# Hybrid decoder layer on one core: first loads on two queues, table load ahead, decay differences on ScalarE

## The chip, the cores and the metric

The kernel runs on one core of one Trainium2 chip. The metric is the time of one execution on the device, in microseconds (us). The engines are named as in the profile: PE (TensorE matmuls), PEld (its weight loads), DVE (VectorE), ACT (ScalarE), POOL (GpSimd) and SP (SyncE, which issues transfers).

## The reference

One decoder layer over 512 tokens of width 1024, in float32:

```python
h = x
h = h + 0.5 * swiglu(rmsnorm(h, g1), w_gate_up, w_down)          # first feed-forward, 2816 wide
proj = rmsnorm(h, g) @ w_in                                      # mixers
y_a = short_conv_branch(b, c, v); y_b = mamba2_branch(z, xbc, dt)
h = h + (sigmoid(g_a) * y_a + sigmoid(g_b) * y_b) @ w_mix_out
h = h + memory_cross_attention(rmsnorm(h, gx), rmsnorm(mem, gm))
h = h + 0.5 * swiglu(rmsnorm(h, g2), ...)                        # second feed-forward
out = rmsnorm(h, gf)
```

The part of the mamba2 branch that the change touches, per head and per chunk of 128 tokens, with `acs` the running sum of `dt * a` (never rising, since a is negative):

```python
seg = acs[..., :, None] - acs[..., None, :]
decay = exp(where(causal, seg, -inf))
y_diag = einsum('bcgls,bcgkls,bcsgkp->bclgkp', C_B, decay, x)    # C_B: C times B, per group
```

## The kernel before, in words

Activations lie with channels on the 128 partitions and the 512 tokens along the row. Every float32 product is made of three matmuls of rounded parts: each operand is split into `hi` and `lo` (`split`, L102: ACT copies to `hi`, DVE subtracts to get `lo`), and a product is hi·hi + hi·lo + lo·hi (L130 to L132 in `job`, L212 to L215 in `mm3`). Weights come from HBM in pieces of 128x1024 through `load_w` (L109): the transfer to tile `wr` is issued by SP, then ACT and DVE split it to `wh` and `wl`. Each of the three tags has three buffers. The order of the instructions on each engine is set when the kernel is built, by a scheduler; on the chip each engine goes through its own list in order.

**Start.** SP issues, in this order: `prm` (all small parameters, L85), the input tile `h0` (L173), the first weight piece in two halves of 128x512 (L115), `h1`, `h2` (L176), the second weight piece (L115), `h3` to `h7` (L179) and the constants `con` (L180). `gained` (L134) multiplies each `h[k]` by its gain and splits it: ACT makes `uh` (L139), DVE `ul` (L140). The first matmuls (L212) need `uh0` and the first half of `wh`. The norm itself (`rms`, L143) is applied behind the matmuls.

**Mixers.** For each of 4 groups of 8 heads, `ssd_out` (L513) goes through 4 pairs of heads (i = 0 to 3). For each head of a pair a transfer by SP spreads the 512 values of `acs` over all partitions into a tile `m` (L520, from the scratch tensor `acd`; four buffers, so the heads of pairs 2 and 3 reuse those of pairs 0 and 1). POOL subtracts `acs` by partition (L522), ACT takes Relu of the negated difference (L525) and then Exp of its negative (L526), DVE multiplies by the masked C·B tile `cb` (L527), and eight small matmuls of 64x128 a pair use it (L539). Three more matmuls (L544) make the part that comes from earlier chunks, scaled by `ea`, which ACT makes with Exp (L533). DVE joins the parts in `yg` (L548, L550), multiplies by the gate (L556), and after four pairs `rms` sums the squares (L150 on ACT, L154 on DVE) and PE adds them over partitions (L158). Matmuls of the next projections (called projection matmuls here, output `pj`) stand between these small ones on PE. The pairs 2 and 3 of a group, with its norm, are called its late half.

Of the kernel before, what the change touches and what calls it, by code (L numbers as in the profile page):

```python
# [62 lines left out]
def layer(ctx: ExitStack, tc: tile.TileContext, a, out):  # L63
# [18 lines left out]
        return psp.tile([P, T], F32, tag=tag, name=nm(tag), bufs=PJ if tag == "pj" else 8 - PJ)  # L82

    prm = cst.tile([P, NCOL], F32, tag="prm", name="prm")
    nc.sync.dma_start(out=prm, in_=a["prm"])  # L85
    h = [hp.tile([P, T], F32, tag=f"h{k}", name=f"h{k}") for k in range(KD)]
    xv = a["xT"].rearrange("(k p) t -> k p t", p=P)
    con = cst.tile([P, 3, P], F32, tag="con", name="con")
    ident, ones, triu = con[:, 0, :], con[:, 1, :], con[:, 2, :]
    eps = cst.tile([P, 1], F32, tag="eps", name="eps")  # L90
    V.memset(eps, EPS)


    cst.tile([P, 8], F32, tag="fill", name="fill")
    small = lambda tag, n, bufs: cst.tile([P, n], F32, tag=tag, name=nm(tag), bufs=bufs)

    ahead = []
# [11 lines left out]
    def load_w(src, n, parts=1):  # L109
        if ahead:  # L110
            return ahead.pop(0)
        raw, hi, lo = ring("wr", F32), ring("wh"), ring("wl")
        for i in range(parts):
            c = slice(i * n // parts, (i + 1) * n // parts)
            nc.sync.dma_start(out=raw[:, c], in_=src[:, c])  # L115
            split(raw[:, c], hi[:, c], lo[:, c])
        return hi, lo
# [16 lines left out]
    def gained(src, gname, k, pool, tag="u", bufs=8, n=T):  # L134

        hi = pool.tile([P, n], F32R, tag=tag + "h", name=nm("uh"), bufs=bufs)
        lo = pool.tile([P, n], F32R, tag=tag + "l", name=nm("ul"), bufs=bufs)
        g = pc(gname, k)
        S.activation(out=hi, in_=src, func=AF.Copy, scale=g)  # L139
        V.scalar_tensor_tensor(out=lo, in0=src, scalar=g, in1=hi, op0=ALU.mult, op1=ALU.subtract)  # L140
        return hi, lo
# [28 lines left out]
        S.copy(out=r, in_=p2[:, :n_tok])  # L170
        return r

    nc.sync.dma_start(out=h[0], in_=xv[0])  # L173
    first = [load_w(a["w_gu1"][0][:, :8 * P], 8 * P, 2)]
    for k in range(1, 3):
        nc.sync.dma_start(out=h[k], in_=xv[k])  # L176
    first.append(load_w(a["w_gu1"][0][:, 8 * P:], 8 * P))
    for k in range(3, KD):
        nc.sync.dma_start(out=h[k], in_=xv[k])  # L179
    nc.sync.dma_start(out=con, in_=a["con"].rearrange("p (a b) -> p a b", a=3))  # L180
    ahead.extend(first)

    up = ctx.enter_context(tc.tile_pool(name="up", bufs=1))
# [4 lines left out]
    def ffn(gname, wgu, wd, fin=None):  # L188
# [2 lines left out]
        ts = ExitStack()  # L191
        tp = ts.enter_context(tc.tile_pool(name=nm("tp"), bufs=1, reuse_waits="tile"))
        tp.tile([P, 48], F32, tag="lag", name=nm("lag"))
        u = [gained(h[k], gname, k, up) for k in range(KD)]
        tq = []
        s = {}

# [186 lines left out]
    with tc.tile_pool(name="mx", bufs=1, reuse_waits="tile") as mx:  # L384
# [128 lines left out]
        def ssd_out(g, ct, xs, cb, xdt, prev):  # L513
            yg = []
            for i in range(4):
                h0 = 8 * g + 2 * i
                ms = []
                for hh in range(2):
                    m = mt("m", MB)
                    DQ.dma_start(out=m, in_=acd_h[h0 + hh].partition_broadcast(P))  # L520
                    m4 = m.rearrange("p (c l) -> p c l", c=NC)
                    G.tensor_tensor(out=m4, in0=m4,  # L522
                                    in1=acs[:, (h0 + hh) * NC:(h0 + hh + 1) * NC].unsqueeze(2)
                                    .to_broadcast([P, NC, P]), op=ALU.subtract)
                    S.activation(out=m, in_=m, func=AF.Relu, scale=-1.0)  # L525
                    S.activation(out=m, in_=m, func=AF.Exp, scale=-1.0)  # L526
                    V.tensor_tensor(out=m, in0=m, in1=cb, op=ALU.mult)  # L527
                    ms.append(m)
                ea = mt("ea", 2)
                for hh in range(2):  # L530
                    DQ.dma_start(out=ea[64 * hh:64 * hh + 64, :],
                                 in_=acd_h[h0 + hh].partition_broadcast(64))
                S.activation(out=ea, in_=ea, func=AF.Exp)  # L533
                yd = ps("ss")
                for c in range(NC):
                    cs = slice(c * P, (c + 1) * P)
                    for hh in range(2):
                        q0 = (2 * i + hh) * 64
                        TE.matmul(yd[64 * hh:64 * hh + 64, cs], xdt[c][:, q0:q0 + 64], ms[hh][:, cs],  # L539
                                  start=True, stop=True)  # L540
                yo = ps("ss")
                for c in range(1, NC):
                    cs = slice(c * P, (c + 1) * P)
                    TE.matmul(yo[:, cs], prev[c - 1][:, i * P:(i + 1) * P], ct[:, cs],  # L544
                              start=True, stop=True)
                V.tensor_tensor(out=ea[:, P:], in0=yo[:, P:], in1=ea[:, P:], op=ALU.mult)
                y = mt("yg", 4)
                V.scalar_tensor_tensor(out=y, in0=xs[i], scalar=pc("ssm_d", 4 * g + i), in1=yd,  # L548
                                       op0=ALU.mult, op1=ALU.add)
                V.tensor_tensor(out=y[:, P:], in0=y[:, P:], in1=ea[:, P:], op=ALU.add)  # L550
                yg.append(y)
            return yg
# [365 lines left out]
```

## Time and profile before

| what | value |
|---|---|
| time, median of 3 runs | 1591.48 us (1591.46 to 1591.81) |
| time of the profiled execution | 1592.54 us |
| its span, first to last instruction | 1590.8 us |
| PE busy | 1557.4 us (98%) |
| DVE, ACT, POOL busy | 1056.0, 733.7, 52.7 us |
| granted clock of TensorE, mean | 0.995 |

The busy time of an engine is what its instructions cover; waits, branches and the issuing of transfers are not counted. A share of the whole span hides what single stretches do, so the stretches where PE stands still are read one by one.

### The profile page before, as it was taken

What the parts mean: (1) busy time and instruction counts of PE and PEld (TensorE: products, weight loads), DVE (VectorE), ACT (ScalarE), POOL (GpSimd) and SP (SyncE); (2) the same over time, 40 slices, a digit from 0 to 9 for tenths busy, and PEclk for the clock granted to TensorE, in tenths of its full rate; (3) what the DMA queues carried; (4) which work ended last, traced back from release to release, by engine and by line L of the source; (5) the groups of instructions that cost most, each with busy time, mean ns of one, the idle gap of its engine ahead of it and who ended that gap; (6) DMA issues with size and microseconds to landing.
All of it is one profiled execution on the core that took longest, in us unless ns stands there. A gap on an engine that the chain in (4) does not pass through costs nothing.

```text
span 1590.8 us, 20744 instructions
## 1 busy us (share of the span) xinstructions
PE 1557.4 (98%) x8253; PEld 1318.0 (83%) x8253; DVE 1056.0 (66%) x1502; ACT 733.7 (46%) x1008; POOL 52.7 (3%) x54
## 2 busy tenths in 40 slices
PE   7999999999989999899999999999999999999997
PEld 6888988987778777787888888888888898998986
DVE  6856856777684877958565544565556876666765
ACT  7432433445768593765332233344344642342343
POOL 0000000002020200201000000000000000000000
PEclk9999999999999999999999999999999999999999
DMA  5432333245242423323242322235204233233221
GB/s 196 133 93 93 98 112 100 66 132 188 93 133 80 138 75 117 122 93 108 78 146 93 105 94 93 95 105 185 93 27 130 83 120 107 93 95 111 86 62 71
DMA packets 53920, 168.70 MB, mean 106 GB/s; under 512 B 6320, under 2 KB 6832, under 8 KB 53824
## 3 DMA queue, kind: packets, MB, share of 16 engines
q1 hardware_dynamic: 51952, 161.03, 31.8%
q0 software_dynamic: 1584, 5.31, 0.9%
q8 instruction: 64, 1.05, 0.3%
q10 hardware_dynamic: 288, 1.05, 0.2%
q14 instruction: 32, 0.26, 0.1%
HBM read 163.10 MB, written 4.26 MB: 105 GB/s over the span
## 4 chain that ended last, share of the span: by engine, by line
PE 55%; DVE 2%; issue 1%; ACT 1%; DMA 0%; DVEq 0%; ACTq 0%
PE pj L132 12%; PE pj L131 12%; PE pj L130 12%; PE pj L212 5%; PE pj L214 5%; PE pj L215 5%; DMA ea<-acd 0%; PE pj L676 0%; PE pj L678 0%; PE pj L677 0%; PE ss L539 0%; DVE wl L104 0%; PE ss L758 0%; ACT wh L103 0%; PE ss L721 0%
## 5 line engine op out<-in xcount | busy, mean ns | idle before, releaser
L103 ACT CAST wh<-wr 128x1024 fp32r<-128x1024 f32 (+2 forms) x250 | 243.6, 975 | 479.9 <-PE pj L131 332.2
L104 DVE TENSOR_TENSOR wl<-wr,wh 128x1024 fp32r<-128x1024 f32 (+2 forms) x250 | 282.0, 1129 | 112.6 <-ACT wh L103 111.0
L130 PE MATMUL pj<-uh,wh 128*128 128x512 f32 (+1 forms) x712 | 281.2, 395 | 0.0
L132 PE MATMUL pj<-uh,wl 128*128 128x512 f32 (+1 forms) x712 | 280.4, 394 | 0.0
L131 PE MATMUL pj<-ul,wh 128*128 128x512 f32 (+1 forms) x712 | 279.5, 393 | 0.0
L212 PE MATMUL pj<-uh,wh 128*128 128x512 f32 (+1 forms) x416 | 153.3, 369 | 8.3 <-ACT wh L103 7.1
L132 PEld LDWEIGHTS pj<-uh,wl 128*128 128x128 f32 (+1 forms) x712 | 133.9, 188 | 29.0 <-issue 0.7
L130 PEld LDWEIGHTS pj<-uh,wh 128*128 128x128 f32 (+1 forms) x712 | 133.8, 188 | 28.6 <-issue 0.9
L131 PEld LDWEIGHTS pj<-ul,wh 128*128 128x128 f32 (+1 forms) x712 | 134.0, 188 | 27.8
L214 PE MATMUL pj<-ul,wh 128*128 128x512 f32 (+1 forms) x416 | 152.4, 367 | 0.0
L215 PE MATMUL pj<-uh,wl 128*128 128x512 f32 (+1 forms) x416 | 151.9, 366 | 0.0
L130 PE MATMUL pj<-sh,wh 128*128 128x512 f32 x346 | 135.3, 391 | 0.1
L131 PE MATMUL pj<-sl,wh 128*128 128x512 f32 x346 | 135.1, 390 | 0.2
L132 PE MATMUL pj<-sh,wl 128*128 128x512 f32 x346 | 134.8, 390 | 0.0
L212 PEld LDWEIGHTS pj<-uh,wh 128*128 128x128 f32 x416 | 78.6, 189 | 22.6 <-ACT wh L103 7.1
L214 PEld LDWEIGHTS pj<-ul,wh 128*128 128x128 f32 x416 | 79.0, 190 | 13.1 <-DVE ul L140 0.5
L215 PEld LDWEIGHTS pj<-uh,wl 128*128 128x128 f32 x416 | 78.5, 189 | 12.8 <-DVE wl L104 0.2
L131 PEld LDWEIGHTS pj<-sl,wh 128*128 128x128 f32 x346 | 65.0, 188 | 14.5 <-DVE sl L104 1.5
L130 PEld LDWEIGHTS pj<-sh,wh 128*128 128x128 f32 x346 | 65.0, 188 | 14.0 <-ACT sh L103 0.9
L132 PEld LDWEIGHTS pj<-sh,wl 128*128 128x128 f32 x346 | 65.0, 188 | 13.4
L352 DVE SCALAR_TENSOR_TENSOR dn<-pj,r 128x512 f32<-128x512 f32 x47 | 32.4, 690 | 57.2 <-PE pj L132 56.9
L381 DVE SCALAR_TENSOR_TENSOR cv<-cx,prm,cv 128x511 f32<-128x511 f32 (+2 forms) x72 | 62.1, 866 | 3.4 <-ACT cv L378 3.1
(278 smaller groups left out, 3088.6 us busy)
## 6 DMA issues: line engine op xcount, KB each, us to landing
wr<-in_w_in SPq DMA_DIRECT2D x80, 512.0 KB, 3.2
wr<-in_w_gu SPq DMA_DIRECT2D x63, 512.0 KB, 3.8
wr<-in_w_d SPq DMA_DIRECT2D x32, 512.0 KB, 3.5
db<-in_w_gu SPq DMA_DIRECT2D x24, 512.0 KB, 3.8
m<-acd SPq DMA_DIRECT2D x32, 256.0 KB, 3.9
wr<-in_w_os SPq DMA_DIRECT2D x32, 256.0 KB, 3.1
wr<-in_w_d SPq DMA_DIRECT2D x16, 384.0 KB, 3.2
ea<-acd SPq DMA_DIRECT2D x32, 128.0 KB, 4.4
```

Source lines behind the costliest of these rows:

```text
L103: S.copy(out=hi, in_=src)
L104: V.tensor_tensor(out=lo, in0=src, in1=hi, op=ALU.subtract)
L130: TE.matmul(pt, hi[:, s_], xh, start=(k == 0), stop=False)
L131: TE.matmul(pt, hi[:, s_], xl, start=False, stop=False)
L132: TE.matmul(pt, lo[:, s_], xh, start=False, stop=(k == nk - 1))
L212: TE.matmul(pt, hi[:, c], xh, start=start and k == 0, stop=False, skip_group_check=True)
L214: TE.matmul(pt, hi[:, c], xl, start=False, stop=False, skip_group_check=True)
L215: TE.matmul(pt, lo[:, c], xh, start=False, stop=stop and k == 3, skip_group_check=True)
L352: V.scalar_tensor_tensor(out=dn, in0=pd, scalar=0.5, in1=r, op0=ALU.mult, op1=ALU.mult)
L381: V.scalar_tensor_tensor(out=acc[:, d:], in0=x[:, :T - d], scalar=pc(wname, j0 + j), in1=acc[:, d:], op0=ALU.mult, op1=ALU.add)
```

## The change

The start: SP issues `prm`, then the first quarter of the first 128x2048 of weights, `h1`, the second quarter, `h4`, the third and fourth quarters, `h5` to `h7` and `con`. ACT issues `h0`, then loads its function table for a copy of one value per partition into a spare tile, then issues `h2` and `h3`. The quarters are split between the `gained` steps (after k = 0, 2, 3 and 5). The mixers: POOL's subtraction is gone; ACT makes Relu(acs - m) in four pieces of 128x128 per head, each with its own column of `acs` as the bias by partition.

```diff
-    nc.sync.dma_start(out=prm, in_=a["prm"])
     xv = a["xT"].rearrange("(k p) t -> k p t", p=P)
+    S.dma_start(out=h[0], in_=xv[0])
+    nc.sync.dma_start(out=prm, in_=a["prm"])
...
-    cst.tile([P, 8], F32, tag="fill", name="fill")
+    warm = cst.tile([P, 8], F32, tag="fill", name="fill")[:, 0:1]
+    S.activation(out=warm, in_=eps, func=AF.Copy, scale=eps)
...
-    nc.sync.dma_start(out=h[0], in_=xv[0])
-    first = [load_w(a["w_gu1"][0][:, :8 * P], 8 * P, 2)]
-    for k in range(1, 3):
-        nc.sync.dma_start(out=h[k], in_=xv[k])
-    first.append(load_w(a["w_gu1"][0][:, 8 * P:], 8 * P))
-    for k in range(3, KD):
+    def load_first(src):
+        return ring("wr", F32), ring("wh"), ring("wl"), src
+    def piece(t, i, eng):
+        raw, hi, lo, src = t
+        c = slice(i * 512, (i + 1) * 512)
+        eng.dma_start(out=raw[:, c], in_=src[:, c])
+        return lambda: split(raw[:, c], hi[:, c], lo[:, c])
+    f0, f1 = load_first(a["w_gu1"][0][:, :1024]), load_first(a["w_gu1"][0][:, 1024:])
+    jobs = [piece(f0, 0, nc.sync)]
+    nc.sync.dma_start(out=h[1], in_=xv[1])
+    S.dma_start(out=h[2], in_=xv[2])
+    jobs.append(piece(f0, 1, nc.sync))
+    S.dma_start(out=h[3], in_=xv[3])
+    nc.sync.dma_start(out=h[4], in_=xv[4])
+    jobs += [piece(f1, 0, nc.sync), piece(f1, 1, nc.sync)]
+    for k in range(5, KD):
         nc.sync.dma_start(out=h[k], in_=xv[k])
     nc.sync.dma_start(out=con, in_=a["con"].rearrange("p (a b) -> p a b", a=3))
+    first = [f0[1:3], f1[1:3]]
...
-        u = [gained(h[k], gname, k, up) for k in range(KD)]
+        u = []
+        for k in range(KD):
+            u.append(gained(h[k], gname, k, up))
+            if jobs and k in (0, 2, 3, 5):
+                jobs.pop(0)()
...
-                    m4 = m.rearrange("p (c l) -> p c l", c=NC)
-                    G.tensor_tensor(out=m4, in0=m4,
-                                    in1=acs[:, (h0 + hh) * NC:(h0 + hh + 1) * NC].unsqueeze(2)
-                                    .to_broadcast([P, NC, P]), op=ALU.subtract)
-                    S.activation(out=m, in_=m, func=AF.Relu, scale=-1.0)
+                    for c in range(NC):
+                        col = (h0 + hh) * NC + c
+                        S.activation(out=m[:, c * P:(c + 1) * P], in_=m[:, c * P:(c + 1) * P],
+                                     func=AF.Relu, scale=-1.0, bias=acs[:, col:col + 1])
                     S.activation(out=m, in_=m, func=AF.Exp, scale=-1.0)
```

The scheduler orders all engines anew. ACT at the start, before (L139 is `uh`, L103 the split of weights):

```order
L139 ACT_TABLE_LOAD
L139 ACTIVATE uh_120<-h_71,prm 128x512
L103 CAST wh_85<-wr_84 128x512 x2
L139 ACTIVATE uh_124<-h_72,prm 128x512
L139 ACTIVATE uh_128<-h_73,prm 128x512
L150 ACTIVATE sq_202<-h_71 128x512
```

and after (L87, L188 and L190 are the transfers, L142 is `uh`, L106 the split):

```order
L87 DMA h_70<-in_xT 128x512
L97 ACT_TABLE_LOAD
L97 ACTIVATE fill<-eps 128x1
L188 DMA h_72<-in_xT 128x512
L190 DMA h_73<-in_xT 128x512
L142 ACTIVATE uh_116<-h_70,prm 128x512
L106 CAST wh_86<-wr_85 128x512
L142 ACTIVATE uh_122<-h_71,prm 128x512
L142 ACTIVATE uh_126<-h_72,prm 128x512
L106 CAST wh_86<-wr_85 128x512
```

The table load stands ahead of everything that waits for data, and `uh` of `h1` and `h2` now stands before the second split of weights.

ACT in the late half of group 0, before (L525 Relu, L526 Exp, L533 Exp of `ea`):

```order
L525 ACTIVATE m_3926<-m_3926 128x512
L526 ACT_TABLE_LOAD
L526 ACTIVATE m_3926<-m_3926 128x512
L525 ACTIVATE m_3932<-m_3932 128x512
L525 ACTIVATE m_3959<-m_3959 128x512
L526 ACTIVATE m_3932<-m_3932 128x512
L533 ACTIVATE ea_3938<-ea_3938 128x512
L526 ACTIVATE m_3959<-m_3959 128x512
L525 ACTIVATE m_3965<-m_3965 128x512
```

and after (L543 Relu, L545 Exp, L552 Exp of `ea`):

```order
L543 ACTIVATE m_3938<-m_3938,keep 128x128 x4
L543 ACTIVATE m_3946<-m_3946,keep 128x128
L545 ACT_TABLE_LOAD
L545 ACTIVATE m_3938<-m_3938 128x512
L543 ACTIVATE m_3946<-m_3946,keep 128x128 x3
L552 ACTIVATE ea_3954<-ea_3954 128x512
L545 ACTIVATE m_3946<-m_3946 128x512
L543 ACTIVATE m_3975<-m_3975,keep 128x128 x4
L543 ACTIVATE m_3983<-m_3983,keep 128x128
L545 ACTIVATE m_3975<-m_3975 128x512
```

Five small Relu pieces stand before the first Exp, where one large Relu stood. In the whole program ACT's table loads go from 74 to 59.

PE at the first use of pair 2 in group 0, before (L539 uses `m`, L544 is the part of earlier chunks, `pj` are projection matmuls):

```order
L130 MATMUL pj_4125<-uh_3262,wh_4127 128x512
L131 MATMUL pj_4125<-ul_3263,wh_4127 128x512
L539 MATMUL ss_3942<-m_3926,xdt_3817 64x128
L544 MATMUL ss_3951<-ct_3501,prev_3823 128x128
L544 MATMUL ss_3951<-ct_3501,prev_3836 128x128
L544 MATMUL ss_3951<-ct_3501,prev_3850 128x128
L132 MATMUL pj_4125<-uh_3262,wl_4128 128x512
L539 MATMUL ss_3942<-m_3932,xdt_3817 64x128
```

and after (L558 uses `m`, L563 is the part of earlier chunks):

```order
L135 MATMUL pj_4145<-uh_3266,wl_4148 128x512
L558 MATMUL ss_3958<-m_3938,xdt_3821 64x128
L563 MATMUL ss_3967<-ct_3505,prev_3827 128x128
L563 MATMUL ss_3967<-ct_3505,prev_3840 128x128
L563 MATMUL ss_3967<-ct_3505,prev_3854 128x128
L133 MATMUL pj_4145<-uh_3270,wh_4147 128x512
L134 MATMUL pj_4145<-ul_3271,wh_4147 128x512
L135 MATMUL pj_4145<-uh_3270,wl_4148 128x512
L133 MATMUL pj_4145<-uh_3274,wh_4147 128x512
L134 MATMUL pj_4145<-ul_3275,wh_4147 128x512
L135 MATMUL pj_4145<-uh_3274,wl_4148 128x512
L133 MATMUL pj_4145<-uh_3278,wh_4147 128x512
```

Seven projection matmuls stand where one stood. Counted from PE's list, the projection matmuls before the first `m` matmul of pair 2; between it and that of the pair's second head; before pair 3; between its two heads; before the sums of squares (L158):

| group | before | after |
|---|---|---|
| 0 | 23, 1, 10, 1, 34 | 22, 7, 3, 7, 21 |
| 1 | 23, 1, 10, 1, 34 | 25, 6, 4, 6, 24 |
| 2 | 23, 1, 10, 1, 34 | 23, 4, 7, 4, 21 |
| 3 | 20, 3, 2 (with both heads), 3, 27 | 21, 4, 7, 4, 23 |

The number of matmuls is the same in both kernels. In the first feed-forward L158 comes after 61 matmuls instead of 63.

## Rows read from the trace of the kernel before

**Rows 1.** The page, busy time by engine.
```profile
PE 1557.4 (98%) x8253; PEld 1318.0 (83%) x8253; DVE 1056.0 (66%) x1502; ACT 733.7 (46%) x1008; POOL 52.7 (3%) x54
```
**Rows 2.** Waits of PE: who waited for whom, total us, times, longest.
```profile
PE ss L539 <- DVE m L527: 8.3, 4, 2.7
PE pj L212 <- ACT wh L103: 7.1, 1, 7.1
PE ss L158 <- DVE sq L154: 4.6, 3, 1.7
```
**Rows 3.** Windows: length, busy PE, PEld, DVE, ACT, POOL; clock, DMA share, GB/s.
```profile
447.50:450.91 3.41, 3.41 (x21) 2.96 (x21) 2.33 (x4) 3.38 (x6) 0.00 (x0) 0.50 0.00 0
```
**Rows 4.** Timeline of the start: start us, us, engine line op [idle before <-releaser].
```profile
1.66 0.90 SPq L115 DMA_DIRECT2D wr<-in_w_gu  x2
...
4.09 1.28 ACT L139 ACT_TABLE_LOAD   x1 [4.09 <-DMA h<-in_xT]
...
6.43 0.62 ACT L103 CAST wh<-wr 128x512 fp32r<-128x512 f32 x1 [0.33 <-DMA wr<-in_w_gu]
```
**Rows 5.** Timeline of the start, ACT and PE after the first matmuls.
```profile
8.51 0.62 ACT L103 CAST wh<-wr 128x512 fp32r<-128x512 f32 x1 [1.46 <-DMA wr<-in_w_gu]
9.17 1.39 ACT L139 ACTIVATE uh<-h,prm 128x512 fp32r<-128x512 f32 x2
...
9.94 0.79 PE L212 MATMUL pj<-uh,wh 128*128 128x512 f32 x1 [1.19 <-ACT uh L139]
...
11.75 0.63 PE L212 MATMUL pj<-uh,wh 128*128 128x512 f32 x1
```
**Rows 6.** Windows: the start, and the first feed-forward.
```profile
4.00:6.00 2.00, 0.00 (x0) 0.00 (x0) 0.00 (x0) 1.90 (x2) 0.00 (x0) 1.00 0.70 137
30.00:50.00 20.00, 20.00 (x90) 16.51 (x89) 19.03 (x31) 15.25 (x20) 0.00 (x0) 1.00 0.25 78
```
**Rows 7.** Timeline, late half of group 0: POOL, DVE, ACT and PE.
```profile
440.64 5.25 POOL L522 TENSOR_TENSOR m<-m,keep 128x512 f32<-128x512 f32 x4 [38.74 <-DMA m<-acd]
...
439.14 0.55 DVE L550 TENSOR_TENSOR yg<-yg,ea 128x384 f32<-128x384 f32 x1
...
440.68 1.41 DVE L550 TENSOR_TENSOR yg<-yg,ea 128x384 f32<-128x384 f32 x1
...
446.35 0.68 DVE L527 TENSOR_TENSOR m<-m,cb 128x512 f32<-128x512 f32 x1
...
443.66 0.63 ACT L526 ACTIVATE m<-m 128x512 f32<-128x512 f32 x1
444.20 1.13 ACT L525 ACTIVATE m<-m 128x512 f32<-128x512 f32 x2
...
447.18 0.41 PE L539 MATMUL ss<-m,xdt 128*64 128x128 f32 x2 [2.67 <-DVE m L527]
```
**Rows 8.** Groups of DVE by form (count, busy us, mean ns): taps beside POOL's work, and later.
```profile
L381 DVE SCALAR_TENSOR_TENSOR cv<-cx,prm,cv 128x510 f32<-128x510 f32 x24 | 23.8, 993 | 0.1
...
L381 DVE SCALAR_TENSOR_TENSOR c<-v,prm,c 128x510 f32<-128x510 f32 x8 | 6.0, 750 | 0.3
```
**Rows 9.** Groups of ACT by form: Silu with and without a column, Relu, Exp.
```profile
L443 ACT ACTIVATE xs<-cv,prm 128x512 f32<-128x512 f32 x16 | 11.5, 721 | 1.0 <-DVE cv L381 0.9
...
L509 ACT ACTIVATE z<-z 128x512 f32<-128x512 f32 x16 | 10.1, 632 | 0.8 <-DVE z L508 0.7
...
L525 ACT ACTIVATE m<-m 128x512 f32<-128x512 f32 x32 | 19.4, 621 | 25.6 <-POOL m L522 25.6
...
L424 ACT ACTIVATE m<-m 128x128 f32<-128x128 f32 x1 | 0.3, 310 | 0.0
```
**Rows 10.** Timeline, DVE before PE's first wait in groups 1 and 3.
```profile
544.90 1.39 DVE L527 TENSOR_TENSOR m<-m,cb 128x512 f32<-128x512 f32 x1
...
739.35 0.69 DVE L527 TENSOR_TENSOR m<-m,cb 128x512 f32<-128x512 f32 x1 [0.85 <-ACT m L526]
```
**Rows 11.** Windows: up to the norm of group 1.
```profile
548.00:566.00 18.00, 16.33 (x96) 12.91 (x96) 17.56 (x23) 15.55 (x22) 5.37 (x4) 1.00 0.44 146
```

## The prediction

> **What bounds the kernel.** I read the page first: PE is busy 1557.4 us of the span of 1590.8 [rows 1], so only some 33 us can be won without taking matmuls away. The waits of PE tell where most of them are [rows 2]: 7.1 us before the first matmul, 8.3 us in four waits (one a group) for the decay tile `m` at the start of pair 2, 4.6 us in three waits for the sum of squares at the end of groups 0 to 2. The windows show a cost beside these: three stretches in the mixers, 3.41 us each, in which the granted clock is 0.50, the lower of TensorE's two levels (1.2 of 2.4 GHz) [rows 3] (the row is the first; the others begin at 467.98 and 662.54). Two of the three follow a wait for squares, one the wait of 2.67 us. Each costs 3.41 x 0.5 = 1.7 us, together 5.1. The change works on all of these.
>
> **The start.** ACT's table load of 1.28 us stood behind the wait for `h0`, at 4.09 [rows 4]. Moving it ahead gives nothing by itself: after `uh` the engine stood still 0.33 us more until the first half of the weights had landed, at 6.4, and the split and the first matmul follow that landing. What counts is when the first quarter lands. It is issued second on SP instead of third; two issues took 0.90 us [rows 4], so it goes out 0.45 us sooner. Lower bound 0, since the same bytes (`prm`, `h0`, quarter) must arrive. Upper bound: it lands together with `h0` at 4.09; then `uh` (0.70, half of the 1.39 of two [rows 5]) goes first, the split starts at 4.79 instead of 6.43, 1.6 us sooner. I take 0.45, nearest to the row of the same transfer. ACT's own two later issues (some 0.45 us each, after the table load that may begin at once) end before 4.1, so the wait for `h0` hides them; without that cover they would cost 0.9.
>
> Next, PE stood 1.19 us before 9.94 [rows 5]: `uh` of `h1` had been queued behind the second split (8.51 to 9.13), itself late by 1.46 us. Now `h1` is issued ahead of the second quarter and its `uh` stands ahead of that split, so it can start about when that quarter landed, at 8.5 instead of 9.17: 0.66 us. The dense stream starts that much sooner, so I count 0.7 for both steps (they are one path, not two). The first matmuls go at the lower clock (one still takes 0.63 us at 11.75 [rows 5], while later 90 of them take 20.00 us, 0.22 each [rows 6]). If the clock rises sooner by the same 0.7, half of that is won again: 0.4; if sooner by a stretch as long as those of [rows 3], 1.7. **Start: 1.1 us, between 0 and 4.5** (1.6 + 1.2 + 1.7). The upper end is unlikely to last: between 30 and 50 us DVE is busy 19.03 of 20 us [rows 6], so matmuls that come sooner soon meet DVE's splits and sums.
>
> The issuing engines are one more question. Between 4 and 6 us the 16 DMA engines were busy 0.70 of the time although many transfers had been issued [rows 6]; a second queue that filled them would bring the first quarter 2.0 x 0.30 = 0.6 us sooner still, a total of 1.7 at the start. The Trainium skill, DMA: Bandwidth & Descriptors, section "Issuing engines are not separate DMA queues", says against this that transfers from several engines interleave on the same DMA engines and that only issue time is saved. By that rule the start stays at 1.1 us; no trace here shows two queues at the start.
>
> **POOL's subtraction.** What it costs is not mainly its own time. While POOL ran its four subtractions, 440.64 to 445.89, an add on DVE of 128x384 took 1.41 us; the same add before it took 0.55 [rows 7]. Over all groups the taps of 128x510 took 993 ns in the mixers and 750 ns where POOL was idle [rows 8]. So DVE reached the multiply of `m` only at 446.35, though ACT's Exp had ended at 444.29 [rows 7]: PE waited 2.1 us for DVE's backlog, not for the decay chain. Without POOL, DVE's four steps between 440.68 and 446.35 need at most 0.55 + 3 x 0.75 = 2.8 us, and DVE is free at 443.5.
>
> **ACT's pieces.** No row shows a Relu of 128x128 with a column as bias. A 128x128 activation takes 0.31 us, and a column adds 721 - 632 = 89 ns [rows 9], so 0.40 alone; one behind the other they overlap by about 0.1 (two Relus of 0.62 take 1.13 [rows 7]), so 0.3 each, 0.31 to be safe. Bounds 0.25 and 0.52 (a whole Relu, one behind the other). Per tile 4 x 0.31 = 1.24 instead of 0.52, over 32 tiles about 23 us more ACT; 15 table loads fewer at 1.28 [rows 4] give 19 back. ACT is busy 46% [rows 1], so the totals don't matter; the chain of a tile does. In group 0 the transfer had landed at 440.64. Five pieces 1.55, table 1.28, Exp 0.63: 444.1, as before (444.29). The multiply (0.68) ends at 444.8 instead of 447.03. PE comes 0.2 sooner (22 matmuls instead of 23) and waits 0.5 instead of 2.67: 2.1 us won. Group 2 is the same pattern: 2.3. In group 1 the multiply itself took 1.39 instead of 0.68 [rows 10] and PE comes two matmuls later: 1.5. In group 3 DVE waited 0.85 for ACT [rows 10], so ACT's chain sets the time and only 0.5 is won. Sum 6.4.
>
> For the later heads ACT gets slower: each tile takes 0.72 more, four tiles 2.9, less the 1.3 of POOL's first subtraction (a quarter of 5.25 [rows 7]) that came before: the fourth Exp comes 1.6 later. The new order puts seven, three and seven matmuls between the heads, where one, ten and one stood: 17 x 0.22 = 3.7 us instead of 2.6. By the same reckoning as above PE then waits about 0.2, 0.45 and 0.15 us at these three places in group 0; I take 0.6 a group, 2.5 in all. **First waits: 6.4 - 2.5 = 3.9 us**, between 0 (the pieces give back all) and 8.3.
>
> The queues: nothing on POOL is behind the subtraction that PE needs. ACT now waits itself for the transfer of `m`; behind it stand only the Exps, and ACT stood idle there for POOL before, 25.6 us in all [rows 9]. On SP the `m` transfers of the next group go behind one weight transfer; they are needed late, after the norm.
>
> **The norm's waits.** Up to L158 of group 1 DVE is busy 17.56 of 18 us with 5.37 of POOL beside it [rows 11]. At twice the length beside POOL, half of 5.37, 2.7 us, goes. But L158 also stands earlier: 38 matmuls after pair 2's first instead of 46 in group 0, 40 in group 1, 36 in group 2: 1.8, 1.3 and 2.2 us. The difference is 0.9 + 1.4 + 0.5 = **2.8 us** of the 4.6 [rows 2]; bounds -1.3 (half of the relief of 8.1 us in three groups reaches the sum, against 5.3 that L158 comes sooner) and 4.6.
>
> **The clock.** With the waits mostly under 1 us I take two of the three slow stretches away: **3.4 us**, between 0 and 5.1. Seven waits [rows 2] went with three slow stretches, so not every wait of this size brings one, and no row says what one under 1 us does; I leave one.
>
> **Sum.** 1.1 + 3.9 + 2.8 + 3.4 = 11.2 us. The profiled execution took 1592.54, so 1581.3; the median of the runs is 1.06 lower, so **1580.2 us**. About 0.2% (3.2 us) is what a measurement of this kernel can tell from no change.
>
> **Rivals.**
> *Two queues carry more.* The first quarter and `h1` land with `h0`, and the clock rises sooner: 4.5 instead of 1.1 at the start. For it: DMA engines not full [rows 6]; against: DVE right behind. 1576.8 us. Chance 0.18.
> *The wait moves.* Only half of DVE's relief reaches the sums of squares, because L158 stands earlier, and the slow stretches stay: 1.1 + 3.9 - 1.3 = 3.7 us, 1587.8; with one slow stretch more 2.0, 1589.5. For it: DVE has little free time in the late half even so [rows 11]; against: 8.1 us of relief is more than the 5.3. Chance 0.14.
> *ACT becomes the bound, slower than before.* Place: the 16 pieces of a late half, on the way to the last `m`. If a piece costs 0.52, as much as a Relu of four times its size, the 16 take 3.4 us more than at 0.31, and PE waits for each of them: 13.4 in four groups. The slow stretches then stay, so 13.4 - 11.2 + 3.4 = 5.6 us slower, 1597.1. It decides at 0.31 + (11.2 - 3.4) / 64 = 0.43 us a piece. Against: the 0.31 that a 128x128 takes even alone without a column [rows 9]. Chance 0.04.
> *The start alone doesn't move* (the quarter lands at 6.4 as before): 1581.3 us, inside the forecast.
>
> **Chances and range.** Forecast 0.64, rivals as said. The range for 8 in 10 reaches over the first rival and most of the second: 1573.5 to 1588.5. Faster by over 0.2% 0.85 (forecast and first rival, and a little of the second), within 0.2% 0.11, slower 0.04.
>
> **What would show it.** Right: first matmul near 6.6 us; PE's waits for `m` under 1 us each, their sum under 4.5; taps of 128x510 near 750 ns in the mixers too; one slow stretch or none in the mixers; PE's first matmul of pair 2 released by ACT's chain rather than by DVE's backlog. Wrong: pieces of over 0.45 us, waits at L158 over 2 us, or a clock at 0.50 in three places again.

## The result, and the profile after

| what | before | after |
|---|---|---|
| median of 5 runs | 1591.48 us (1589.77 to 1592.26) | 1583.25 us (1580.82 to 1585.28) |
| profiled execution, its span | 1592.54, 1590.8 us | 1583.25, 1581.5 us |

The ratio is 0.9948 (95% interval 0.9933 to 0.9963): 8.2 us faster by the medians, 9.3 us between the two profiled executions. I forecast 1580.2 and 11.2 us, in a range from 1573.5 to 1588.5. The sign and most of the mechanism hold. The sum does not come about term by term as I wrote it.

The page, busy time of the changed kernel, answers to [rows 1]:

```profile
PE 1556.1 (98%) x8253; PEld 1316.7 (83%) x8253; DVE 1036.4 (66%) x1503; ACT 733.2 (46%) x1091; POOL 10.4 (1%) x22
```

POOL's 42 us of subtractions are gone, DVE does the same work in 19.6 us less, and ACT's total did not move, since fewer table loads pay for the pieces. PE's waits answer to [rows 2] (total us, times, longest):

```profile
PE pj L232 <- ACT wh L106: 7.1, 1, 7.1
PE pj L135 <- DVE wl L107: 3.5, 1, 3.5
PE ss L558 <- DVE m L546: 2.7, 5, 1.5
...
PE ss L479 <- ACT ct L463: 0.9, 1, 0.9
...
PE ss L161 <- DVE sq L157: 0.4, 1, 0.4
```

The waits for `m` fell from 8.3 to 2.7 us. Those for squares at the ends of groups 0 to 2 fell from 4.6 to nothing worth a row: the 0.4 that is listed stands in the first feed-forward, at 23 us, where the kernel before has no such wait. The first wait of 7.1 is what it was. Two rows are new: 3.5 us for `wl` at 655.5, and 0.9 us at 460.9 for `ct`, which ACT makes with Silu for the next group. The windows for the clock answer to [rows 3]:

```profile
447.50:450.91 3.41, 3.41 (x27) 2.66 (x28) 2.90 (x6) 3.38 (x6) 0.00 (x0) 1.00 0.66 222
659.00:662.41 3.41, 3.41 (x8) 2.73 (x9) 3.41 (x4) 3.38 (x7) 0.00 (x0) 0.50 0.60 208
1054.95:1058.37 3.42, 3.34 (x15) 3.34 (x16) 3.42 (x10) 2.03 (x5) 0.00 (x0) 0.50 0.49 158
```

The stretch of [rows 3] is at full clock now. One stretch at 0.50 is left in the mixers, and it stands right behind the new wait for `wl`. Another has come at 1055, behind two waits of 1.26 and 0.66 us for the split of the memory (`mnh`, `mnl`, operands of the cross attention) that the kernel before has too, without a fall.

At the start I expected the first matmul near 6.6 us. The timeline of the changed kernel answers to [rows 4, 5]:

```profile
1.18 1.28 ACT L97 ACT_TABLE_LOAD   x1 [1.18 <-PEq L928]
...
4.01 0.72 ACT L142 ACTIVATE uh<-h,prm 128x512 fp32r<-128x512 f32 x1 [1.24 <-DMA h<-in_xT]
...
6.38 0.62 ACT L106 CAST wh<-wr 128x512 fp32r<-128x512 f32 x1 [1.66 <-DMA wr<-in_w_gu]
...
7.05 0.80 PE L232 MATMUL pj<-uh,wh 128*128 128x512 f32 x1 [7.05 <-ACT wh L106]
7.57 1.34 ACT L142 ACTIVATE uh<-h,prm 128x512 fp32r<-128x512 f32 x2 [0.57 <-DMA h<-in_xT]
...
8.50 0.64 PE L232 MATMUL pj<-uh,wh 128*128 128x512 f32 x1
...
10.54 0.40 PE L234 MATMUL pj<-ul,wh 128*128 128x512 f32 x1
```

The table load is out of the way and `uh` is done 1.3 us sooner, but ACT now waits 1.66 us for the first quarter instead of 0.33. The quarter went out 0.48 us sooner and its split began at 6.38 instead of 6.43. The second step worked: `uh` of `h1` comes ahead of the second split, and the matmul that stood still for 1.19 us in [rows 5] follows without a gap. The last row is the first matmul at the faster pace (0.40 us in the list, 0.23 from one start to the next, where 0.63 and 0.43 stood before it). In the kernel before, the first at that pace is the 13th, 3.6 us later:

```profile
14.18 0.40 PE L215 MATMUL pj<-uh,wl 128*128 128x512 f32 x1
```

In the late half of group 0 the chain of [rows 7] looks like this:

```profile
438.28 1.58 ACT L543 ACTIVATE m<-m,keep 128x128 f32<-128x128 f32 x5 [5.07 <-DMA m<-acd]
...
441.17 0.63 ACT L545 ACTIVATE m<-m 128x512 f32<-128x512 f32 x1
...
441.83 0.69 DVE L546 TENSOR_TENSOR m<-m,cb 128x512 f32<-128x512 f32 x1 [0.61 <-ACT m L545]
...
442.68 0.40 PE L558 MATMUL ss<-m,xdt 128*64 128x128 f32 x2 [0.33 <-DVE m L546]
```

Five pieces in a row take 1.58 us (I had 1.55). Now DVE waits 0.61 us for ACT, where PE waited for DVE's backlog before. The taps (the steps of the short convolution, L381 before, L401 now) answer to [rows 8]:

```profile
L401 DVE SCALAR_TENSOR_TENSOR cv<-cx,prm,cv 128x510 f32<-128x510 f32 x24 | 17.9, 745 | 0.1
```

That is the 750 ns that I expected, down from 993.

The new wait, on the timeline at the border from group 2 to 3:

```profile
652.57 1.06 ACT L106 CAST wh<-wr 128x1024 fp32r<-128x1024 f32 x1 [0.25 <-PE pj L134]
...
655.08 2.73 DVE L401 SCALAR_TENSOR_TENSOR cv<-cx,prm,cv 128x510 f32<-128x510 f32 x4
...
657.72 1.22 DVE L107 TENSOR_TENSOR wl<-wr,wh 128x1024 fp32r<-128x1024 f32 x1
...
658.99 0.79 PE L135 MATMUL pj<-uh,wl 128*128 128x512 f32 x1 [3.48 <-DVE wl L107]
```

`wh` was there at 653.63. DVE had other work in its list first, four taps among it, and began the subtraction for `wl` at 657.72. PE stood still from 655.51 on.

### The profile page after: what moved, and what is told of

Read it like the earlier page. It is cut to its first block, busy times and chain, and to the rows that moved or that the text cites. A ratio compares the mean times of both kernels' runs of the same rounds, so it can differ in the third digit from the quotient of the medians.

```text
span 1581.5 us, 20708 instructions
## 1 busy us (share of the span) xinstructions
PE 1556.1 (98%) x8253; PEld 1316.7 (83%) x8253; DVE 1036.4 (66%) x1503; ACT 733.2 (46%) x1091; POOL 10.4 (1%) x22
## 4 chain that ended last, share of the span: by engine, by line
PE 92%; DVE 3%; DMA 2%; ACT 2%; issue 1%; DVEq 0%; SPq 0%; ACTq 0%
PE pj L135 19%; PE pj L134 19%; PE pj L133 19%; PE pj L232 9%; PE pj L234 9%; PE pj L235 9%; DMA ea<-acd 1%; PE ss L558 1%; PE ss L509 1%; DVE wl L107 1%; ACT wh L106 1%; PE ss L563 1%; PE pj L697 0%; PE pj L696 0%; PE pj L695 0%
## 5 line engine op out<-in xcount | busy, mean ns | idle before, releaser
L106 ACT CAST wh<-wr 128x1024 fp32r<-128x1024 f32 (+2 forms) x251 | 243.8, 972 | 501.9 <-PE pj L134 357.0
L106 ACT CAST wh<-sa 128x1024 fp32r<-128x1024 f32 x24 | 25.3, 1054 | 71.1 <-PE pj L234 39.9
```

The lines of the kernel that those rows point to most:

```text
L106: S.copy(out=hi, in_=src)
```

## The experiments

**The start alone.** The kernel before with the start of the change; in the mixers POOL subtracts as before.

```diff
+    S.dma_start(out=h[0], in_=xv[0])
+    S.activation(out=warm, in_=eps, func=AF.Copy, scale=eps)
...
+    jobs += [piece(f1, 0, nc.sync), piece(f1, 1, nc.sync)]
```

> The start of the change alone (three queues' issues, table load ahead, quarters); POOL keeps its subtraction and ACT its whole Relu. The order of all instructions behind the first feed-forward's start is that of the kernel before. Theory (the start is worth what the trace of the changed kernel shows at the same matmul, 1.8 us, and the rest of the gain is the mixers'): 1.8 us faster than before, 1.2 to 2.4; first matmul at 7.1 as before, no wait before the matmul of h1's `uh`, waits for `m` 8.3 us in four and for squares 4.6 in three. Rival (the start's gain is used up by DVE's backlog in the first feed-forward): under 0.5 us. Rival (two queues carry more and all later stages profit): over 3 us.

(The issuing engines of the start are two, SP and ACT, not three.) Measured: 1591.39 us against 1591.37 before, ratio 0.9998 (0.9988 to 1.0008). By the measured time nothing was won, which is the first rival's figure; its reason is not shown by that. PE's waits in its profile:

```profile
PE ss L559 <- DVE m L547: 9.0, 4, 2.6
...
PE ss L161 <- DVE sq L157: 4.4, 3, 1.9
```

The mixers wait as before, and the 1.19 us gap of the start is gone. So a gain is there in the trace and not in the median; the runs with the early `wl` below take that up.

**The pieces alone.** The start is that of the kernel before.

```diff
-                    G.tensor_tensor(out=m4, in0=m4,
...
-                    S.activation(out=m, in_=m, func=AF.Relu, scale=-1.0)
+                    for c in range(NC):
...
+                                     func=AF.Relu, scale=-1.0, bias=acs[:, col:col + 1])
```

> ACT's pieces alone; the start is that of the kernel before. In the mixers the orders of DVE and ACT are those of the changed kernel. Theory (the two parts add up): 9.3 - 1.8 - 0.2 = about 7 us faster than before (5.5 to 8), with the 3.5 us wait for `wl` at the end of group 2 there again and the clock falling behind it; first matmul 7.1, 1.19 us wait behind it. Rival (the new wait and the clock's fall come from how the two parts meet): the 3.5 us wait is not there and it is 10 to 12 us faster than before.

Measured: 1583.19 us, ratio 0.9940 (0.9926 to 0.9953). That is the whole gain of the change, a little over my 5.5 to 8. Waits of PE:

```profile
PE pj L132 <- DVE wl L104: 3.5, 1, 3.5
...
PE ss L459 <- ACT ct L443: 0.9, 1, 0.9
```

Both new waits come with the pieces, so they are not an effect of the two parts together. The windows have the stretch behind the wait for `wl`, and that behind the two waits for the memory's split:

```profile
658.83:662.24 3.41, 3.41 (x15) 2.83 (x16) 3.41 (x4) 3.38 (x7) 0.00 (x0) 1.00 0.61 180
1050.53:1055.00 4.47, 3.80 (x29) 3.60 (x30) 4.47 (x11) 3.45 (x10) 0.00 (x0) 1.00 0.37 121
```

The clock fell behind neither of them here, though the waits are the same to 0.01 us as in the changed kernel. So the wait alone does not decide whether the clock falls; what else does stays open, and my expectation of a fall was too firm.

**POOL busy again.** The changed kernel, with POOL's subtraction put behind DVE's multiply, into a tile that nothing reads.

```diff
                     V.tensor_tensor(out=m, in0=m, in1=cb, op=ALU.mult)
+                    G.tensor_tensor(out=idle.rearrange("p (c l) -> p c l", c=NC),
+                                    in0=m.rearrange("p (c l) -> p c l", c=NC),
...
+                                    .to_broadcast([P, NC, P]), op=ALU.subtract)
```

> The changed kernel, and POOL does its subtraction again, 32 times 128x512, but behind DVE's multiply of each `m` and into a spare tile that nothing reads; the orders of the other engines stay those of the changed kernel. Theory (what POOL cost was DVE's time beside it): DVE's busy time goes from 1036 back to about 1055 us, taps of 128x510 in the mixers from 745 to over 850 ns, the waits for squares come back, and the time is 3 to 6 us above the changed kernel. Rival (POOL stood on the chain of `m`, and that it is out of the chain is what won): DVE unchanged within 3 us and the time within 1 us of the changed kernel's.

**The same, twice.** Each of these subtractions is issued two times.

> The run with POOL busy again, each of its 32 subtractions done twice, so about 77 us of POOL instead of 38; the orders of the other engines as in the changed kernel. With one it was 2.7 us above the changed kernel and DVE 8.3 us busier. Theory (POOL's work takes DVE's time wherever the two meet): DVE 14 to 18 us busier than in the changed kernel, 4 to 7 us slower. Rival (those 2.7 us came from the clock's falls, not from POOL): time and DVE as in the single one, within 1.5 us.

Measured: 1585.94 us (ratio to before 0.9963, 0.9951 to 0.9975) with one, 2.7 over the changed kernel where I had expected 3 to 6, with intervals that overlap; and 1594.88 (1.0019, 1.0010 to 1.0028) with two, 11.6 over it where I had expected 4 to 7. Their pages, once and twice:

```profile
PE 1558.7 (98%) x8253; PEld 1317.0 (83%) x8253; DVE 1044.7 (66%) x1503; ACT 733.4 (46%) x1091; POOL 49.0 (3%) x54
```

```profile
PE 1558.9 (98%) x8253; PEld 1317.1 (83%) x8253; DVE 1055.9 (66%) x1503; ACT 733.9 (46%) x1091; POOL 92.7 (6%) x86
```

The other engines' orders are those of the changed kernel, and nothing reads what POOL makes. POOL's reads do hold the buffers of `m`: with two, SP waited 8.9 us for them, six times, before it issued the next transfer. That did not reach the chain, since ACT waited 13.2 us for those transfers, and 13.6 in the changed kernel. DVE is 8.3 and 19.5 us busier. With two it is as busy as before the change, 1055.9 us, and all of the gain is lost and a little more. PE's waits with two:

```profile
PE ss L568 <- DVE m L548: 6.3, 9, 1.7
...
PE ss L161 <- DVE sq L157: 2.8, 5, 1.0
PE ss L509 <- DVE xe L505: 2.5, 2, 2.0
```

All three are waits for DVE, 8.5 us more than in the changed kernel (`xe` is an operand of the chunks' state). So POOL beside DVE, outside the chain of `m`, brings PE's waits back through DVE's time. The size does not follow from DVE's total: with one subtraction PE's waits are the changed kernel's within 0.5 us, and of the 3.6 us between the two profiles PE's own busy time is 2.6. That the 2.7 us of one subtraction come from DVE's 8.3 is therefore not shown.

Single taps I had wrong: they stay at 743 ns with one subtraction, since POOL now runs behind the multiply of `m` and meets other two-operand steps, the squares (`sq`, 686 to 750 ns) and the next multiplies (688 to 749). Groups of DVE with POOL doubled (count, busy us, mean ns):

```profile
L548 DVE TENSOR_TENSOR m<-m,cb 128x512 f32<-128x512 f32 x32 | 29.4, 929 | 8.7 <-ACT m L547 8.4
...
L577 DVE SCALAR_TENSOR_TENSOR yg<-xs,prm,ss 128x512 f32<-128x512 f32 x16 | 11.8, 741 | 2.5 <-PE ss L568 2.4
...
L575 DVE TENSOR_TENSOR ea<-ss,ea 128x384 f32<-128x384 f32 x16 | 8.8, 551 | 3.8 <-ACT m L547 1.5 <-ACT ea L562 1.1 <-PE ss L573 0.6
```

The multiply of `m` went from 688 to 929 ns. The two operations that read `ss`, which lies in PSUM, kept their 0.74 and 0.55 us, although 8 of the 16 of each ran beside a POOL subtraction. The Trainium skill, SBUF — State Buffer, section "Who interferes with whom", says that a DVE instruction with two inputs in SBUF contends with a GpSimd instruction that reads SBUF, that one with at most one input there (outside some faster modes) does not, and that the pair of ports they share is an exclusive lock. This trace agrees: a multiply that started beside a POOL subtraction ended 0.54 us after it and took 1.52 us instead of 0.69.

```profile
447.78 1.90 POOL L553 TENSOR_TENSOR idle<-m,keep 128x512 f32<-128x512 f32 x1
...
448.70 1.52 DVE L548 TENSOR_TENSOR m<-m,cb 128x512 f32<-128x512 f32 x1
```

**`prm` issued by POOL.** The first quarter becomes the first transfer on SP.

```diff
-    nc.sync.dma_start(out=prm, in_=a["prm"])
+    G.dma_start(out=prm, in_=a["prm"])
```

> The changed kernel with `prm` issued by POOL: the first quarter of the weights is now the first transfer that SP issues, as `h0` is ACT's. In the changed kernel it was second on SP and landed at 6.4 although it went out 0.5 us sooner. Theory (a queue's second transfer lands some 2.4 us behind its first, whenever issued): the quarter lands at 4.0 to 4.6, the first matmul comes at 5.2 to 5.8, and 1 to 1.9 us are won against the changed kernel, if `prm` lands by 4. Rival (the bytes set it: prm, h0 and the quarter share the same engines): landing 5.4 to 6.4, gain under 0.8. Rival (POOL's issue is late, and `uh` of h0 waits for `prm`): first matmul at 7 or later, slower by 0 to 2 us.

Measured: 1584.62 us, ratio 0.9953 (0.9940 to 0.9965), not to be told from the changed kernel. The start:

```profile
1.26 0.68 POOL L88 DMA_DIRECT2D prm<-in_prm  x1 [0.81 <-POOLq L928]
...
7.61 0.72 ACT L142 ACTIVATE uh<-h,prm 128x512 fp32r<-128x512 f32 x1 [4.83 <-DMA prm<-in_prm]
...
8.89 0.79 PE L232 MATMUL pj<-uh,wh 128*128 128x512 f32 x1 [8.89 <-ACT wh L106]
```

The third theory was right about the path: POOL's transfer landed last, `uh` of `h0` waited for it until 7.61, and the first matmul came at 8.89. The first theory fell too. As first transfers of their queues the quarter took 4.7 us from issue to landing and `h0` 5.0, where `h0` beside the small `prm` took 3.2. That fits transfers that go out together and share the time, as the second theory said; the landing came at its lower end.

**`wl` early.** The changed kernel; one subtraction for `wl` (the projection of the third `xs` of group 3) ranks 80 instructions earlier in the scheduler.

```diff
+                with tc.high_priority(80):
+                    V.tensor_tensor(out=lo[:, c], in0=raw[:, c], in1=hi[:, c], op=ALU.subtract)
```

> The changed kernel; one weight piece (the projection of the third `xs` of group 3) has DVE's subtraction for `wl` put ahead in the scheduler's ranking, which moves instructions of PE, DVE and ACT between the norm of group 2 and the start of group 3 and nowhere else. Theory (the 3.5 us wait for `wl` is one of order: the subtraction stood behind four taps although `wh` was there; the fall of the clock follows from the wait): the wait is gone, no slow stretch near 659, 3.5 to 5.2 us faster than the changed kernel, 1578 to 1579.7. Rival (DVE has no time there, and the wait comes back under another name, for `cx`, `xs` or `m`): 0 to 1.5 us faster, waits of the stretch 640 to 700 us still over 2.5 us.

Measured: 1576.33 us, ratio 0.9904 (0.9890 to 0.9917), 6.9 us below the changed kernel. PE's waits:

```profile
PE ss L567 <- DVE m L555: 1.0, 3, 0.5
PE ss L488 <- ACT ct L472: 0.9, 1, 0.9
```

The wait is gone and nothing took its place: between 640 and 700 us PE is busy all 60.00 us with 272 matmuls, where the changed kernel has 56.52 us and 254. So it was one of order, as the theory had it; the ranking moved neighbours of that subtraction too, so it is the new order that is shown, not the one instruction. The gain is over the theory's upper end of 5.2. A second set of runs gave 1578.92 (ratio 0.9919, 0.9907 to 0.9932; below), so 4.3 to 6.9 us.

**`wl` early with the old start**, and both once more on one chip.

```diff
-    S.dma_start(out=h[0], in_=xv[0])
...
+    first = [load_w(a["w_gu1"][0][:, :8 * P], 8 * P, 2)]
```

> As the run before it, but with the start of the kernel before. It asks again what the start is worth, in a kernel with few waits behind it. Theory (the start wins 1.2 to 1.8 us of PE's waits, but the clock's first rise and the slow stretches fall differently from run to run, so that a median of some runs shows nothing of it): medians within 1.5 us of the run with the new start, no sign of one. Rival (the new start is worth 1.8 us and the run with the start alone hid it by bad luck): 1.8 us slower than the run with the new start. Rival (the new start costs): faster by over 1 us.

> The changed kernel with the early `wl`, once more, beside the same with the old start on the same chip: in the first pair the new start was 2.4 us faster, in the kernels without the early `wl` nothing. If the start is worth its 1.2 to 1.8 us, the two pairs together show 1 to 2.5; if the first pair was chance, this one shows 0 within 1.

> The early `wl` with the start of the kernel before, once more: 1 to 2.5 us slower than the run with the new start if that start is worth what PE's waits say, equal within 1 us if not.

Measured: 1578.71 (0.9917, 0.9904 to 0.9931) against 1576.33 in the first pair, 1580.68 (0.9925, 0.9913 to 0.9938) against 1578.92 in the second. The new start is 2.4 and 1.8 us better; the start alone showed 0.0, and the pieces with and without it 1583.25 and 1583.19. The intervals of each pair overlap. What the traces tell is steadier. In the 12 profiles with either start and `prm` on SP, the first matmul comes at 6.76 to 7.39 us (new) and 6.80 to 7.16 (old). The 101st comes at 30.83 to 32.05 with the new start, 31.5 on average in 7, and at 31.39 to 32.82 with the old, 32.5 on average in 5. That is 0.9 us; the 1.8 of the first pair of profiles was half luck. At the 13th matmul the new start is ahead by 1.2 us on average (12.4 against 13.6), and by 2.5 in the first pair. Such a gain is easily lost in the runs: the 12 runs with the start alone had a mean granted clock of 0.9936, the 17 of before beside them 0.9946, and 0.0010 of 1590 us is 1.6 us. That this covered the gain in the first experiment fits the numbers; why the clock was lower in those runs stays open.

**The order alone.** The changed kernel with the early `wl`; all loads issued by SP again and no table load ahead, but `h1` and its `uh` keep their new places.

```diff
-    S.dma_start(out=h[0], in_=xv[0])
+    nc.sync.dma_start(out=h[0], in_=xv[0])
...
-    S.activation(out=warm, in_=eps, func=AF.Copy, scale=eps)
```

> The changed kernel with the early `wl`, but all loads are issued by SP again and the table load stands again behind the wait for `h0`; the quarters, `h1` ahead of the second quarter and its `uh` ahead of the second split stay. Theory (of the start only the order of `uh` of h1 and the second split counts; two issuing engines and the table load ahead move nothing on PE's path): first matmul at 7.1 within 0.4, no idle time over 0.4 us before the matmul of h1's `uh`, the 13th matmul (index 12) at 11.7 to 13, and the median within 1 us of the kernel with both queues. Rival (the queues count): first matmul at 7.6 or later, and 1 to 2 us slower than with both queues.

Measured: 1576.55 us, ratio 0.9908 (0.9895 to 0.9921), 2.4 us below the same kernel with both queues on that chip and 0.2 above that kernel's first runs, on another. Its start:

```profile
4.10 1.28 ACT L147 ACT_TABLE_LOAD   x1 [4.10 <-DMA h<-in_xT]
...
6.62 0.62 ACT L106 CAST wh<-wr 128x512 fp32r<-128x512 f32 x1 [0.50 <-DMA wr<-in_w_gu]
...
7.29 0.79 PE L237 MATMUL pj<-uh,wh 128*128 128x512 f32 x1 [7.29 <-ACT wh L106]
...
8.74 0.63 PE L237 MATMUL pj<-uh,wh 128*128 128x512 f32 x1
```

The first matmul comes at 7.29 (7.27 and 7.39 with both queues in the same kernel), there is no gap before `h1`'s matmul, and the 101st comes at 31.30. Of the whole start, two issuing engines and the early table load move nothing; the new places of `h1` and its `uh` (with the quarters, which stayed) do it. The rule of the Trainium skill that I weighed (DMA: Bandwidth & Descriptors, section "Issuing engines are not separate DMA queues"), that issuing from several engines saves only the time of the issuing, agrees with this pair of traces, and even that time was hidden.

**Eight pieces.** The changed kernel with Relus of 128x64.

```diff
-                    for c in range(NC):
+                    for c in range(2 * NC):
+                        col, half = (h0 + hh) * NC + c // 2, slice(c * 64, (c + 1) * 64)
```

> The changed kernel with eight Relus of 128x64 instead of four of 128x128 per head. A piece of 128x128 took 0.33 us in a row; of 128x64 I estimate 0.25 to 0.28, so a head's chain is 0.7 to 0.9 us longer, ACT 22 to 30 us busier. Theory (ACT's chain now sets PE's first waits for `m` of a group, so any length added to it is paid there): waits for `m` from 2.7 us to 6 to 10, 3 to 7 us slower than the changed kernel. Rival (DVE and PE's own order set them, ACT has slack): waits for `m` under 4 us, time within 1.5 us.

Measured: 1589.26 us, ratio to before 0.9979 (0.9969 to 0.9989), 6.0 us over the changed kernel. ACT is 32.7 us busier, 0.26 us a piece. Waits of PE:

```profile
PE ss L509 <- ACT btok L489: 2.1, 1, 2.1
PE pj L135 <- DVE wl L107: 2.0, 1, 2.0
PE ss L171 <- DVE rb L167: 1.8, 1, 1.8
PE ss L509 <- DVE xe L505: 1.5, 1, 1.5
...
PE ss L558 <- DVE m L546: 1.2, 2, 1.0
```

The size was in my range and the place was not. The waits for `m` even fell, and PE waits for `btok`, `xe`, `rb` and `wl` instead: the scheduler put pieces ahead of other work of ACT (between 418.84 and the copy of `btok` at 424.41 stand seven of them, 1.77 us, with two table loads; `btok` is the other operand of the chunks' state, `rb` holds the norm's factors). ACT at 48% busy has no slack that the average promises. Between the two profiles the loss is 4.2 us of span, and 2.8 of it is PE's busy time (1558.9 against 1556.1 for the same matmuls): the granted clock was 0.50 from 425.14 to 431.97, behind the wait for `btok`, and from 462.69 to 469.52. How much of the 6.0 is the pieces' time and how much the new order was not separated.

**No subtraction at all.** The kernel before, where ACT's Relu takes the transferred values as they are.

```diff
-                    G.tensor_tensor(out=m4, in0=m4,
...
-                                    .to_broadcast([P, NC, P]), op=ALU.subtract)
```

> The kernel before without POOL's subtraction and without ACT's pieces: ACT's one Relu of 128x512 takes the transferred values as they are. It leaves out the subtraction of `acs` by partition. So it has what taking the work off POOL gives, at no price on ACT (32 times 4 pieces of 0.33 us against 32 Relus of 0.6, some 24 us of ACT); the scheduler's order may move. Theory (DVE's relief is the gain, and ACT's pieces cost a part of it): DVE near 1036 us, and 2 to 5 us faster than the pieces alone (1583.2), so 1578 to 1581. Rival (ACT has the room, the pieces cost nothing on PE's path): within 1.5 us of the pieces alone. Rival (the gain came from where the new order puts the matmuls, not from POOL): 1587 or more.

Measured: 1576.00 us, ratio 0.9898 (0.9879 to 0.9916), 7.2 us below the pieces alone; I had expected 2 to 5. Its page:

```profile
PE 1551.9 (99%) x8253; PEld 1314.5 (84%) x8253; DVE 1034.8 (66%) x1502; ACT 718.9 (46%) x997; POOL 10.4 (1%) x22
```

DVE has the same relief, PE waits 3.1 us for `m` and nowhere for `wl` or `ct`. So by the medians taking the work off POOL, with the order that the scheduler found without it, was worth 15.5 us, and the pieces, with theirs, gave 7.2 back. The early `wl` wins 4.3 to 6.9 us in the changed kernel by order, so most of these 7.2 need not be ACT's time. The two profiles show less of a difference: they are 2.6 us apart (1574.2 and 1576.8 of span), the pieces' being the fastest of their six runs, and in neither does the clock fall in the mixers.

## Why the prediction was right, and where it was not

By its own terms, between the two profiled executions (predicted 11.2, found 9.3):

| term | predicted | found | how |
|---|---|---|---|
| start | 1.1 | 1.8 | the 101st matmul, 32.82 to 31.01; 0.9 over 12 profiles |
| waits for `m`, net | 3.9 | 5.6 | 8.3 to 2.7 |
| norm's waits | 2.8 | 4.6 | 4.6 to none |
| clock | 3.4 | 1.7 | three stretches in the mixers became one, one came at 1055 |
| new waits for `wl` and `ct` | none | -4.4 | 3.5 and 0.9 |

The rows add up to 9.3 partly by luck. They leave out two small waits that went (0.5 for `ea`, 0.4 for `xe`) and a slower end: the clock fell at 1573.8 with matmuls to go until 1575.2, and in the kernel before only after the last one.

- **DVE's relief** was the heart of the forecast, and the mechanism is shown: as much slowing of DVE, put back at other places with no order moved, brought back 8.5 us of PE's waits and took the whole gain. A rival is that POOL stood in the chain of `m` itself. In the trace of the kernel before, 9.9 of the 12.9 us of these waits ended with DVE's backlog and not with the chain: in groups 0 and 2 the multiply began 2.06 us after ACT's Exp, and the last squares 2.7 to 3.0 us after ACT's own, with DVE busy all that time. In group 1 the two came within 0.1 us of each other, and in group 3 the chain was last. My sizes were too small. The first waits of pair 2 fell from 8.3 to 0.8 us, where I had 1.9 left; group 0's from 2.67 to 0.33, where I had 0.5; and the squares of groups 0 to 2 lost all of their wait.
- **The pieces' price** was right as a duration: 0.33 us each over all 128 (42.1 us), against 0.31, and no rival of 0.43 or more. The 2.5 us for new waits at the later heads were about right in sum (2.0) and not in kind: I had many of under half a microsecond, and there were two, 0.55 in group 1 and 1.47 in group 3.
- **The step that failed** is the one on the queues: "nothing on POOL is behind the subtraction that PE needs", and behind ACT's wait "stand only the Exps". I asked what stands behind POOL, ACT and SP, and not what the new order does at the borders of two groups, where nobody touched the code. There 4.4 us went, 3.5 through DVE's list (`wl`) and 0.9 through ACT's (`ct`), and in this profile a fall of the clock with them. Group 3 has another wait of ACT that I did not look at: two pieces of `m` stood behind its wait of 2.41 us for the transfer of `ea` (1.14 us in the kernel before), and PE waited 1.47 us:

```profile
731.51 0.63 ACT L552 ACTIVATE ea<-ea 128x512 f32<-128x512 f32 x1 [2.41 <-DMA ea<-acd]
732.05 0.68 ACT L543 ACTIVATE m<-m,keep 128x128 f32<-128x128 f32 x2
...
734.14 0.40 PE L558 MATMUL ss<-m,xdt 128*64 128x128 f32 x2 [1.47 <-DVE m L546]
```

- **The start** had two steps for one path. The first ("it goes out 0.45 us sooner", and so lands sooner) failed in whole: the quarter landed at 6.4 as before, which the text kept as the last rival. The second (`uh` of `h1` ahead of the second split) was enough for the size that I gave. In this pair the faster pace of the matmuls began 3.6 us sooner, where I had counted 0.7; 2.5 us were won by the 13th matmul and 1.8 were left at the 101st, so later stages did take a part back, as I had said of the upper end.
- **The clock** was mis-sized, being counted as if certain. By the runs of the two kernels the mean granted clock went from 0.9946 (17 runs) to 0.9958 (5 runs), and 0.0012 of 1590 us is about 1.9 us, not 3.4.
- **The rivals.** "Two queues carry more" is out: the order alone does as well. "The wait moves" had the right idea and the wrong place: a wait did take the place of those removed, but for `wl`, and the one at the norm went away. "ACT becomes the bound" did not come at 0.33 us a piece.
- **The signs.** Two of those named for a right forecast were missed: the first matmul came at 7.05 and not near 6.6, and one wait for `m` was over 1 us. The sum of these waits, the taps, the one stretch in the mixers and the release of pair 2 by ACT's chain came as said.

The forecast came out 3 us from the measured median because what was missed (4.4 us of new waits, 1.7 of the clock) was made up in good part by what was underrated (3.5 in the two groups of waits, 0.7 at the start). That these nearly cancel is luck.

## What to carry to other kernels

Where two engines slow each other, price the helper by what the other loses beside it (19.6 us of DVE for 42 us of POOL here), look at which operands the slowed instructions read, and at who waits for them: 8.3 us of DVE's time put back elsewhere added under 0.5 us to PE's waits. When a scheduler orders the work, a cheaper or dearer instruction moves others, so read the new order at the borders between stages, on engines that the change doesn't touch; ranking one subtraction higher was worth at least half as much as the change. At a start, first ask what the first wait ends with: here it was a transfer's landing, which an issue 0.5 us sooner moved by 0.05.

## What was not expected of the hardware

The same wait brings a fall of the clock in one run and none in another: 3.48 us before `wl` were followed by 3.41 us at 0.50 in the changed kernel and by none in the pieces alone; 1.26 and 0.67 us at 1050 to 1065 by one in the changed kernel and by none in the kernel before. Even one and the same kernel differs: of the two profiles of the early `wl`, one has 3.41 us at 0.50 behind these two waits, from 1049.47 on, and the other has none. So one profile's count of such stretches is a sample. The runs of one kernel spread over some 7 us (before: 1588.28 to 1595.20 among 9), and much of that goes with the mean granted clock, which was 0.997 in the fastest run and 0.991 to 0.995 in the four slowest.
